# Adding the two halves of the attention's values by an accumulating transfer to DRAM

## The chip, the cores and the metric

The kernel runs on one core of a Trainium2 chip. The metric is the device time of one execution in microseconds (us), as the median of several runs. The engines are PE (TensorE, the matrix products), DVE (VectorE), ACT (ScalarE), POOL (GpSimd) and SP (SyncE, which here only issues transfers). Each engine works through its own queue in order and waits at semaphores for the others. Transfers are issued from SP's queue and, for some loads, from POOL's.

## The reference

Two layers (DEPTH = 2) run over 2048 latent tokens and 256 context tokens of width 1024. Each layer has multi-head latent attention with 8 heads (64 + 32 columns of query and key, 64 of value), a short convolution and a longer one; their outputs, each with a gate, go together through an output projection. Cut to the attention and what follows it:

```python
def one_block(qi):
    s = jnp.einsum('bqhd,bkhd->bhqk', qi, k).astype(jnp.float32) * sm_scale
    p = jax.nn.softmax(s, axis=-1).astype(v.dtype)
    return jnp.einsum('bhqk,bkhd->bqhd', p, v)
...
y_a = attn * jax.nn.silu(g_a)
...
return jnp.concatenate([y_a, y_b, y_c], axis=-1)
...
x <- x + gate * (y @ w_out[l])
```

In the last layer only the latent tokens are needed.

## The kernel before

Everything is in f32. To keep its precision, a product takes each operand as a rounded upper part and the remainder (names with h and l at the end: woh and wol, yh and yl, ph and pl), and the helper `mm3` makes three products of them (L194 to L196). The helper `split` makes the two parts: a cast on ACT (L190), then the subtraction of the remainder on POOL or DVE (L191).

Each layer has four stages: tokens, features, attention, project. The stages overlap at their ends: the project stage is written after the attention, but a raised priority lets its first part start 8 pairs (AE) before the attention ends.

**Attention.** Jobs run over 8 heads and, in each, over 4 blocks of 512 queries (layer 0 has a block of 256 context queries per head besides). A job walks through the 18 tiles of 128 keys in 9 pairs. For a pair PE makes the scores sc (L1080 to L1082), ACT takes two exponentials of them (p at L1083, the rounded ph at L1084), POOL subtracts the one from the other (pl, L1085), DVE adds p to the sums acc in PSUM (L1092), and, one pair later, PE multiplies ph and pl with the values (L1107, L1108) into po. The maxima of the next blocks are made ahead: PE makes a product pmax (L992), and DVE reduces it (mx, L993). The values stand in Vt with 128 columns: 64 of their upper part and 64 of the remainder. So po has 128 rows, and the attention's output is the sum of its rows 0 to 63 and 64 to 127.

The last pair of a job is followed by `close`: ACT copies the sums (accs, L1112) and po (o, L1114), SP stores o to DRAM (o_d, L1115), PE transposes the sums (L1120), and DVE makes their reciprocals (rinv, L1122 and L1123). What is to follow a pair is held in a list `late`, which `flush` empties after the next pair's subtraction.

**Project.** `prepare_w` loads a column of the output weights (wraw, L1150) and splits it into woh and wol. `prepare_y` loads, for one block of tokens, the gated outputs of the convolutions (L1170) and, per pair of heads k, both halves of o_d: the upper one into yr (L1175), the lower one into ylo (L1176), each in two transfers of 64 rows, and the gate yg (L1177). ACT and PE spread rinv over the rows (prr, L1181 and L1182). DVE then adds ylo to yr (L1183), multiplies by prr (L1184) and by the gate (L1185), and the result is split into yh and yl. The products pout (L194 to L196) follow; DVE adds them to the residual xo (L1213). In layer 0 the squares are summed for the next layer's norm, with the variance va at L1236 and its spreading on PE at L1243.

The order of each queue is not written out. A scheduler places all instructions by their priorities and its own estimate of times, and so a change in one place can move rows on any engine.

Of the kernel before, what the change touches and what calls it, by code (L numbers as in the profile page):

```python
# [9 lines left out]
F32 = mybir.dt.float32  # L10
# [3 lines left out]
ALU = mybir.AluOpType  # L14
# [4 lines left out]
P = 128  # L19
# [4 lines left out]
NT = SEQ + CTX  # L24
NTT = NT // P
DEPTH = 2
H = 8
NOPE, ROPE, DV, QK = 64, 32, 64, 96
# [56 lines left out]
def trunk(ctx: ExitStack, tc: tile.TileContext, ins, out):  # L85
    nc = tc.nc
    V, S, G, PE = nc.vector, nc.scalar, nc.gpsimd, nc.tensor

    def pool(stack, name, **kw):
        return stack.enter_context(tc.tile_pool(name=name, bufs=kw.pop("bufs", 1), **kw))  # L90
# [3 lines left out]
    dr = pool(ctx, "dr", space=DRAM)  # L94

    def psum(tag, name):
        return ps.tile([P, 512], F32, tag=tag, name=name, bufs={"a": 3, "b": 2}.get(tag, 1))
# [54 lines left out]
    v_d = [dr.tile([H, P, NTT, P], F32, name=f"v_d{l}") for l in range(DEPTH)]  # L152
    sga_d = [dr.tile([512, NT], F32, name=f"sga_d{l}") for l in range(DEPTH)]
    sgc_d = [dr.tile([256, NT], F32, name=f"sgc_d{l}") for l in range(DEPTH)]
    o_d = [dr.tile([H, P, NT], F32, name=f"o_d{l}") for l in range(DEPTH)]
    y_d = [dr.tile([512, NT], F32, name=f"y_d{l}") for l in range(DEPTH)]
    x1_d = dr.tile([D, NT], F32, name="x1_d")
    xs = [ins["xT"], x1_d]
# [780 lines left out]
    def attention(l, start):  # L939
# [3 lines left out]
        op = pool(es, f"Ao{l}", reuse_waits="tile", side="right")  # L943
# [29 lines left out]
        def bank(name):  # L973
            turns[0] += 1
            return psum("bbe"[turns[0] % 3], name)
# [71 lines left out]
        def use_mods():  # L1047
            while ready:
                i, j, parts = ready.pop(0)
                modulation(i, (j,), lambda _: parts, mp.tile([4, P], F32, tag="mrow", name="mrow", bufs=2))  # L1050


        late = []

        def flush():
            for st in late:
                st()
            late.clear()

        for idx, job in enumerate(jobs):  # L1060
            h = job[0][0]
            if job[0][1] == (1024 if h else 512) and h + 1 < H:
                load(h + 1)
            pairs = [(j, it) for j in job for it in range(j[3], NTT, 2)]
            for pi, ((h, s, n, k0), kt0) in enumerate(pairs):
                if idx == len(jobs) - 1 and pi == len(pairs) - AE:
                    mark = tc.cur_priority
                K, Vt, Q = kv[h]
                first, final = kt0 == k0, kt0 == NTT - 2
                if first:  # L1070
                    po = psum("c", "po")
                    acc = psum("d", "acc")
                p = tp.tile([P, 2, 512], F32, tag="p", name="p", bufs=4)
                ph = tp.tile([P, 2, 512], F32R, tag="ph", name="ph", bufs=3)
                pl = tp.tile([P, 2, 512], F32R, tag="pl", name="pl", bufs=3)
                scs = []
                for z in range(2):
                    kt, qt = kt0 + z, slice(s // P, (s + n) // P)
                    sc = psum("a", "sc")
                    PE.matmul(sc[:, :n], lhsT=K[0:97, kt, 0], rhs=Q[0:97, qt, 0], start=True, stop=False)  # L1080
                    PE.matmul(sc[:, :n], lhsT=K[0:QK, kt, 0], rhs=Q[0:QK, qt, 1], start=False, stop=False)  # L1081
                    PE.matmul(sc[:, :n], lhsT=K[0:QK, kt, 1], rhs=Q[0:QK, qt, 0], start=False, stop=True)  # L1082
                    S.activation(p[:, z, :n], sc[:, :n], AF.Exp, scale=scale)  # L1083
                    S.activation(ph[:, z, :n], sc[:, :n], AF.Exp, scale=scale)  # L1084
                G.tensor_tensor(pl[:, :, :n], p[:, :, :n], ph[:, :, :n].bitcast(F32), op=ALU.subtract)  # L1085
                flush()

                for z in range(2):
                    if first and z == 0:
                        V.tensor_copy(acc[:, :n], p[:, 0, :n])  # L1090
                    else:
                        V.tensor_tensor(acc[:, :n], acc[:, :n], p[:, z, :n], op=ALU.add)  # L1092
                for z in range(2):
                    at = pi + (z + 1) / 2 + LEAD
                    if at <= len(pairs):
                        ahead(idx + 1, at / len(pairs))
                    else:
                        ahead(idx + 1, 1)
                        ahead(idx + 2, (at - len(pairs)) / len(pairs))
                if pi == len(pairs) // 2:  # L1100
                    split_mods()
                if pi == len(pairs) - ME:
                    use_mods()

                def products(kt0=kt0, n=n, Vt=Vt, ph=ph, pl=pl, po=po, first=first, final=final):
                    for z in range(2):
                        PE.matmul(po[:, :n], lhsT=Vt[:, kt0 + z, :], rhs=ph[:, z, :n], start=first and z == 0, stop=False)  # L1107
                        PE.matmul(po[:, :n], lhsT=Vt[:, kt0 + z, :], rhs=pl[:, z, :n], start=False, stop=final and z == 1)  # L1108

                def close(h=h, s=s, n=n, po=po, acc=acc):  # L1110
                    accs = op.tile([P, 512], F32, tag="o", name="accs", bufs=3)
                    S.activation(accs[:, :n], acc[:, :n], AF.Copy, scale=2.0)  # L1112
                    o = op.tile([P, 512], F32, tag="o", name="o", bufs=3)
                    S.copy(o[:, :n], po[:, :n])  # L1114
                    nc.sync.dma_start(o_d[l][h, :, s : s + n], o[:, :n])  # L1115

                    nq = n // P
                    px = bank("psum_t")
                    for t in range(nq):
                        PE.transpose(out=px[:, t * P : (t + 1) * P], in_=accs[:, t * P : (t + 1) * P], identity=idn)  # L1120
                    sm = tp.tile([P, 4], F32, tag="sm", name="sm", bufs=2)
                    V.tensor_reduce(sm[:, :nq], px[:, :n].rearrange("p (t k) -> p t k", k=P), axis=AX.X, op=ALU.add)  # L1122
                    V.reciprocal(rinv[l][:, s // P : s // P + nq, h], sm[:, :nq])  # L1123

                late.append(products)
                if final:
                    late.append(close)
        if not AE:
            mark = tc.cur_priority
        flush()  # L1130
        if not last:
            assert not mods and not ready
            gains(l + 1)
# [4 lines left out]
    def project(l, start):  # L1138
# [3 lines left out]
        op = pool(es, f"Oo{l}", reuse_waits="tile", side="right")  # L1142
        rp = pool(es, f"Or{l}", reuse_waits="tile", side="right")
# [17 lines left out]
        def prepare_y(bi):  # L1161
            s, n = blocks[bi]
            where = (ap, bp)[bi % 2]
            yh = where.tile([P, KD, 512], F32R, tag="yh", name="yh")[:, :, :n]
            yl = where.tile([P, KD, 512], F32R, tag="yl", name="yl")[:, :, :n]
            ys[bi] = (yh, yl)
            for k in order:
                r = rp.tile([P, 512], F32, tag="yr", name="yr", bufs=4)
                if k >= 4:
                    nc.sync.dma_start(r[:, :n], y_d[l][(k - 4) * P : (k - 3) * P, s : s + n])  # L1170
                else:
                    lo = rp.tile([P, 512], F32, tag="ylo", name="ylo", bufs=2)
                    g = rp.tile([P, 512], F32, tag="yg", name="yg", bufs=2)
                    for z in range(2):
                        nc.sync.dma_start(r[64 * z : 64 * z + 64, :n], o_d[l][2 * k + z, 0:64, s : s + n])  # L1175
                        nc.sync.dma_start(lo[64 * z : 64 * z + 64, :n], o_d[l][2 * k + z, 64:128, s : s + n])  # L1176
                    nc.sync.dma_start(g[:, :n], sga_d[l][k * P : (k + 1) * P, s : s + n])  # L1177
                    px = psum("b" if bi == 0 else "cde"[k % 3], "prr")
                    for t in range(n // P):
                        rr = rp.tile([P, 2, 64], F32, tag="rr", name="rr", bufs=RR)  # L1180
                        S.copy(rr, rinv[l][:, s // P + t, 2 * k : 2 * k + 2].unsqueeze(2).to_broadcast([P, 2, 64]))  # L1181
                        PE.transpose(out=px[:, t * P : (t + 1) * P], in_=rr.rearrange("p a b -> p (a b)"), identity=idn)  # L1182
                    V.tensor_tensor(r[:, :n], r[:, :n], lo[:, :n], op=ALU.add)  # L1183
                    V.tensor_tensor(r[:, :n], px[:, :n], r[:, :n], op=ALU.mult)  # L1184
                    V.tensor_tensor(r[:, :n], r[:, :n], g[:, :n], op=ALU.mult)  # L1185
                split(yh[:, k, :n], yl[:, k, :n], r[:, :n], V if bi == 0 and (SPV & 4 and k < 4 or SPV & 8 and k >= 4) else None)
                yield
# [129 lines left out]
```

## Time and profile before

| | before |
|---|---|
| median of 3 runs | 3669.24 us (3668.04 to 3670.11) |
| the profiled execution | 3673.98 us |
| its span | 3672.2 us |
| mean granted clock of PE | 0.977 of 2.4 GHz |
| busy PE, DVE, POOL, ACT | 96%, 78%, 64%, 59% |
| moved by DMA, mean rate | 411.47 MB, 112 GB/s |

The profile is of one execution, by the hardware's own records. A row of the groups gives engine, operation and tiles (out<-in, buffer numbers left out), the count, then the busy time in us and the mean ns of one, then the time the engine stood idle just before such instructions and what ended it. A row of a timeline gives start and duration in us; several equal instructions in a row stand as xN, with their time together; square brackets give the idle time before it and its releaser. The span falls into these parts: layer 0's attention from 822 to about 1740 us, its projection up to about 1980, layer 1's tokens and features up to about 2620, its attention up to 3490 and its projection up to the end.

### The profile page before, as it was taken

Reading aid. Unit: us, or ns where it says so; the run is one execution under the profiler, and the core shown is the slowest. Engines: PE = TensorE matmul, PEld = TensorE weight load, DVE = VectorE, ACT = ScalarE, POOL = GpSimd, SP = SyncE. Lnnn points to the kernel's source line nnn. Section 1 sums busy time; section 2 is a strip of 40 time slices with the busy share of each in tenths; the row PEclk is TensorE's granted clock in tenths of the full one; section 3 lists DMA queues with packets and bytes.
Section 4 is the critical chain, followed back from the end, with each engine's and each line's share of the span. In section 5 each row is a group of like instructions: output and inputs, shape, how many; then the busy total and the mean of one; then the engine's idle time right before and its main releaser. Section 6 shows DMA issues by size and latency. Waiting matters only on the chain. (4 is left out here: it accounts for less than half of the span.)

```text
span 3672.2 us, 52697 instructions
## 1 busy us (share of the span) xinstructions
PE 3513.0 (96%) x17532; PEld 2913.7 (79%) x17532; DVE 2870.1 (78%) x5472; ACT 2167.6 (59%) x4328; POOL 2343.4 (64%) x1497
## 2 busy tenths in 40 slices
PE   7899999999999999999999989999999999999999
PEld 5787888887888888877788878887677888887777
DVE  6986977777888888887436879678988898888932
ACT  5665343337777877777445663433567777777720
POOL 4664344348888888887335664544678888887721
PEclk9899999999999999999999999999999999999999
DMA  7567333533333223311766773435241122222173
GB/s 220 172 186 208 82 108 103 119 105 88 80 80 80 50 65 80 87 55 46 239 216 208 219 225 91 132 91 134 66 97 29 43 62 59 62 59 72 40 207 115
DMA packets 394386, 411.47 MB, mean 112 GB/s; under 512 B 19168, under 2 KB 332128, under 8 KB 388960
## 3 DMA queue, kind: packets, MB, share of 16 engines
q1 hardware_dynamic: 387712, 333.87, 31.3%
q0 software_dynamic: 6400, 74.22, 8.9%
q8 instruction: 138, 2.26, 0.3%
q14 instruction: 136, 1.11, 0.1%
HBM read 266.72 MB, written 141.59 MB: 111 GB/s over the span
## 5 line engine op out<-in xcount | busy, mean ns | idle before, releaser
L1085 POOL TENSOR_TENSOR pl<-p,ph 128x1024 fp32r<-128x1024 f32 (+1 forms) x584 | 1389.4, 2391 | 262.4 <-ACT ph L1084 158.7
L1083 ACT ACTIVATE p<-sc 128x512 f32<-128x512 f32 x1168 | 704.7, 605 | 291.6 <-PE sc L1082 276.2
L993 DVE TENSOR_REDUCE mx<-pmax 128x1 fp32r<-128x512 f32 (+1 forms) x1296 | 787.0, 628 | 111.7 <-PE pmax L992 106.8
L1092 DVE TENSOR_TENSOR acc<-acc,p 128x512 f32<-128x512 f32 x1096 | 757.1, 691 | 66.8 <-ACT p L1083 44.8
L1084 ACT ACTIVATE ph<-sc 128x512 fp32r<-128x512 f32 x1168 | 698.3, 605 | 20.1 <-PE po L1107 16.4
L194 PE MATMUL pf<-hhf,wh 128*128 128x256 f32 (+1 forms) x1584 | 549.3, 348 | 16.8 <-ACT tg L867 8.3
L196 PE MATMUL pf<-hhf,wl 128*128 128x512 f32 (+1 forms) x1584 | 546.7, 347 | 3.9 <-POOL wl L191 2.9
L195 PE MATMUL pf<-hlf,wh 128*128 128x256 f32 (+1 forms) x1584 | 548.0, 346 | 0.2
L1080 PE MATMUL sc<-Q,K 97*128 97x512 f32 x1168 | 473.3, 405 | 8.6 <-ACT ph L1084 8.4
L992 PE MATMUL pmax<-K,Q 96*128 96x512 f32 (+1 forms) x1296 | 453.4, 384 | 26.4 <-DVE mx L993 19.6
L1108 PE MATMUL po<-pl,Vt 128*128 128x512 f32 x1168 | 466.3, 400 | 1.7 <-POOL pl L1085 1.0
L1081 PE MATMUL sc<-Q,K 96*128 96x512 f32 x1168 | 465.2, 398 | 0.0
L1107 PE MATMUL po<-ph,Vt 128*128 128x512 f32 x1168 | 461.1, 395 | 1.4 <-DMA Vt<-v_d 0.8
L1082 PE MATMUL sc<-Q,K 96*128 96x512 f32 x1168 | 462.0, 396 | 0.0
L191 POOL TENSOR_TENSOR wl<-wraw,wh 128x1024 fp32r<-128x1024 f32 x104 | 253.9, 2442 | 296.3 <-ACT wh L190 283.5
L747 DVE SCALAR_TENSOR_TENSOR cacc<-z,hv,cacc 128x384 f32<-128x384 f32 (+5 forms) x780 | 403.2, 563 | 14.3 <-ACT cacc L742 11.2
L194 PEld LDWEIGHTS pf<-hhf,wh 128*128 128x128 f32 x1584 | 303.9, 192 | 55.1 <-ACT tg L867 8.9
L196 PEld LDWEIGHTS pf<-hhf,wl 128*128 128x128 f32 x1584 | 303.4, 192 | 44.1 <-POOL wl L191 6.8
L195 PEld LDWEIGHTS pf<-hlf,wh 128*128 128x128 f32 x1584 | 304.2, 192 | 36.9 <-POOL hlf L191 0.6
L992 PEld LDWEIGHTS pmax<-K,Q 96*128 96x128 f32 x1296 | 244.7, 191 | 94.7 <-DVE mx L993 37.0
L1080 PEld LDWEIGHTS sc<-Q,K 97*128 97x128 f32 x1168 | 222.3, 190 | 61.6 <-ACT ph L1084 16.1
L1082 PEld LDWEIGHTS sc<-Q,K 96*128 96x128 f32 x1168 | 224.5, 192 | 51.4
(257 smaller groups left out, 6179.9 us busy)
## 6 DMA issues: line engine op xcount, KB each, us to landing
wraw<-in_w_in SPq DMA_DIRECT2D x108, 512.0 KB
q_d<-sg SPq DMA_DIRECT2D x68, 384.0 KB
wm<-in_w_mod SPq DMA_DIRECT2D x46, 512.0 KB
v_d<-vs SPq DMA_DIRECT2D x36, 512.0 KB
kn_d<-sg SPq DMA_DIRECT2D x72, 256.0 KB
K<-kn_d POOLq DMA_DIRECT2D x16, 1152.0 KB, 8.5
Vt<-v_d POOLq DMA_DIRECT2D x16, 1152.0 KB, 15.1
o_d<-o SPq DMA_DIRECT2D x64, 256.0 KB
```

The costliest lines, as they stand in the source:

```text
L194: PE.matmul(out_, lhsT=ahi, rhs=bhi, start=first, stop=False)
L195: PE.matmul(out_, lhsT=ahi, rhs=blo, start=False, stop=False)
L196: PE.matmul(out_, lhsT=alo, rhs=bhi, start=False, stop=last)
L992: PE.matmul(pm[:, :w], lhsT=Q[0:QK, s // P + t, 0], rhs=K[0:QK, a // P : (a + w) // P, 0], start=True, stop=True)
L993: V.tensor_reduce(part[:, t, c : c + 1], pm[:, :w], axis=AX.X, op=ALU.max)
L1080: PE.matmul(sc[:, :n], lhsT=K[0:97, kt, 0], rhs=Q[0:97, qt, 0], start=True, stop=False)
L1082: PE.matmul(sc[:, :n], lhsT=K[0:QK, kt, 1], rhs=Q[0:QK, qt, 0], start=False, stop=True)
L1083: S.activation(p[:, z, :n], sc[:, :n], AF.Exp, scale=scale)
L1084: S.activation(ph[:, z, :n], sc[:, :n], AF.Exp, scale=scale)
L1085: G.tensor_tensor(pl[:, :, :n], p[:, :, :n], ph[:, :, :n].bitcast(F32), op=ALU.subtract)
L1092: V.tensor_tensor(acc[:, :n], acc[:, :n], p[:, z, :n], op=ALU.add)
L1108: PE.matmul(po[:, :n], lhsT=Vt[:, kt0 + z, :], rhs=pl[:, z, :n], start=False, stop=final and z == 1)
```

## The change

The buffer o_d shrinks from 128 rows a head to 64. SP stores only the upper half of o. The lower half is added to it in DRAM by a transfer with `accum_op=ALU.add`, issued on POOL's queue. It can be issued only once the store has landed, so it is held in a list `adds` and issued by the third `flush` from the one that runs `close`, two pairs after it. In the project stage the loads of ylo, the tile and the addition L1183 are gone.

```diff
-    o_d = [dr.tile([H, P, NT], F32, name=f"o_d{l}") for l in range(DEPTH)]
+    o_d = [dr.tile([H, DV, NT], F32, name=f"o_d{l}") for l in range(DEPTH)]
...
+        adds = []
+
         def flush():
             for st in late:
                 st()
             late.clear()
+            for a in list(adds):
+                a[0] -= 1
+                if a[0] < 0:
+                    a[1]()
+                    adds.remove(a)
...
-                    nc.sync.dma_start(o_d[l][h, :, s : s + n], o[:, :n])
+                    nc.sync.dma_start(o_d[l][h, :, s : s + n], o[0:DV, :n])
+
+                    adds.append([2, lambda: G.dma_start(o_d[l][h, :, s : s + n], o[DV:P, :n], accum_op=ALU.add)])
...
-        flush()
+        while late or adds:
+            flush()
...
-                    lo = rp.tile([P, 512], F32, tag="ylo", name="ylo", bufs=2)
                     g = rp.tile([P, 512], F32, tag="yg", name="yg", bufs=2)
                     for z in range(2):
-                        nc.sync.dma_start(r[64 * z : 64 * z + 64, :n], o_d[l][2 * k + z, 0:64, s : s + n])
-                        nc.sync.dma_start(lo[64 * z : 64 * z + 64, :n], o_d[l][2 * k + z, 64:128, s : s + n])
+                        nc.sync.dma_start(r[64 * z : 64 * z + 64, :n], o_d[l][2 * k + z, :, s : s + n])
...
-                    V.tensor_tensor(r[:, :n], r[:, :n], lo[:, :n], op=ALU.add)
```

In counts: 72 accumulating transfers come onto POOL (40 in layer 0, 32 in layer 1; 64 of 512 columns and 8 of 256), 72 loads of 64 rows leave SP, 36 additions leave DVE. The new lines shift the numbers below them: in the changed kernel the subtraction pl is L1092, the sums acc L1099, the copies accs and o L1119 and L1121, the store L1122, the accumulation L1124, the loads of yr L1184, the multiplications L1191 and L1192, xo L1220.

Where instructions move: DVE at the end of layer 0's attention, before (yr and ylo belong to the project stage, mx and acc to the attention).

```order
L1123 RECIPROCAL rinv_63<-sm 128x2
L993 TENSOR_REDUCE mx_89<-pmax 128x1 x3
L1092 TENSOR_TENSOR acc<-acc,p 128x512
L993 TENSOR_REDUCE mx_89<-pmax 128x1
L1183 TENSOR_TENSOR yr<-yr,ylo 128x512
L993 TENSOR_REDUCE mx_89<-pmax 128x1
L1183 TENSOR_TENSOR yr<-yr,ylo 128x512
L1092 TENSOR_TENSOR acc<-acc,p 128x512
L993 TENSOR_REDUCE mx_89<-pmax 128x1 x3
```

The same place of the changed kernel:

```order
L1132 RECIPROCAL rinv_63<-sm 128x2
L993 TENSOR_REDUCE mx_89<-pmax 128x1 x2
L1099 TENSOR_TENSOR acc<-acc,p 128x512
L993 TENSOR_REDUCE mx_89<-pmax 128x1 x3
L1099 TENSOR_TENSOR acc<-acc,p 128x512
L993 TENSOR_REDUCE mx_89<-pmax 128x1 x3
L1099 TENSOR_TENSOR acc<-acc,p 128x512
```

The additions that stood between the maxima are gone, and maxima and sums close up.

ACT at the start of layer 1's projection, before (rr and woh and yh belong to the projection, the rest to the attention):

```order
L1181 COPY rr<-rinv_64 128x128 x3
L1112 ACTIVATE accs<-acc 128x512
L190 CAST woh<-wraw 128x1024
L1002 CAST Q<-pmt 1x4x128
L190 CAST yh<-yr 128x512 x2
L1114 COPY o<-po 128x512
L190 CAST yh<-yr 128x512 x2
```

And in the changed kernel:

```order
L1189 COPY rr<-rinv_64 128x128 x3
L1002 CAST Q<-pmt 1x4x128
L1119 ACTIVATE accs<-acc 128x512
L190 CAST woh<-wraw 128x1024
L190 CAST yh<-yr 128x512
L1090 ACTIVATE p<-sc 128x512
L1091 ACTIVATE ph<-sc 128x512
```

The cast of Q, which the next maxima need, has moved ahead of the copy of the sums and of the cast of woh, which waits for a load of weights.

POOL within layer 0's attention, in the changed kernel (wml is a split of modulation weights that runs beside the attention):

```order
L1092 TENSOR_TENSOR pl<-p,ph 128x1024 x5
L1124 DMA o_d_112<-o 64x512
L1092 TENSOR_TENSOR pl<-p,ph 128x1024 x5
L191 TENSOR_TENSOR wml<-wm,wmh 128x1024
L1092 TENSOR_TENSOR pl<-p,ph 128x1024 x4
L1124 DMA o_d_112<-o 64x512
```

Between two accumulations stand nine subtractions pl, one job; before, the same stretch held only the subtractions and the splits.

## Rows read from the trace of the kernel before

**Rows 1.** The page's part 1: busy us (share of the span), instructions.

```profile
PE 3513.0 (96%) x17532; PEld 2913.7 (79%) x17532; DVE 2870.1 (78%) x5472; ACT 2167.6 (59%) x4328; POOL 2343.4 (64%) x1497
```

**Rows 2.** Windows: length, busy us of PE, PEld, DVE, ACT, POOL, clock, DMA share, GB/s.

```profile
830.00:1600.00 770.00, 762.86 (x3783) 614.88 (x3782) 663.15 (x1244) 600.64 (x1129) 673.55 (x306) 1.00 0.30 72
1600.00:1760.00 160.00, 145.33 (x662) 113.00 (x661) 129.05 (x200) 111.37 (x230) 107.56 (x49) 0.94 0.26 80
```

**Rows 3.** Groups by line: count, then busy us, mean ns, then idle before and releasers.

```profile
L1183 DVE TENSOR_TENSOR yr<-yr,ylo 128x512 f32<-128x512 f32 (+1 forms) x36 | 38.3, 1063 | 65.6 <-DMA yr<-o_d 42.4 <-DMA ylo<-o_d 23.0
...
L1085 POOL TENSOR_TENSOR pl<-p,ph 128x1024 fp32r<-128x1024 f32 (+1 forms) x584 | 1389.4, 2391 | 262.4 <-ACT ph L1084 158.7 <-PE pmax L992 27.4 <-PE sc L1082 18.1
...
L1108 PE MATMUL po<-pl,Vt 128*128 128x512 f32 x1168 | 466.3, 400 | 1.7 <-POOL pl L1085 1.0
```

**Rows 4.** Timeline of DVE at the end of layer 0's attention: start, duration.

```profile
1622.63 6.68 DVE L1183 TENSOR_TENSOR yr<-yr,ylo 128x512 f32<-128x512 f32 x1 [0.90 <-DMA yr<-o_d]
1629.24 0.68 DVE L993 TENSOR_REDUCE mx<-pmax 128x1 fp32r<-128x512 f32 x1
1629.84 0.68 DVE L1183 TENSOR_TENSOR yr<-yr,ylo 128x512 f32<-128x512 f32 x1
```

**Rows 5.** Timeline of POOL at the same place.

```profile
1621.78 6.99 POOL L1085 TENSOR_TENSOR pl<-p,ph 128x1024 fp32r<-128x1024 f32 x3
```

**Rows 6.** Timeline of PE: five waits, and a reading of pl.

```profile
1629.97 0.58 PE L992 MATMUL pmax<-K,Q 96*128 96x256 f32 x1 [5.65 <-DVE mx L993]
...
1812.93 0.47 PE L1243 MATMUL prs<-idr,rep 128*128 128x128 f32 x2 [3.57 <-DVE rep L1242]
...
3367.58 0.80 PE L992 MATMUL pmax<-K,Q 96*128 96x512 f32 x1 [1.02 <-ACT Q L1002]
...
3385.95 1.10 PE L992 MATMUL pmax<-K,Q 96*128 96x512 f32 x2 [2.65 <-DVE mx L993]
...
3438.89 0.40 PE L1108 MATMUL po<-pl,Vt 128*128 128x512 f32 x1
...
3547.78 0.50 PE L194 MATMUL pout<-yh,woh 128*128 128x512 f32 x1 [1.24 <-DVE xo L1213]
```

**Rows 7.** Windows at three clock dips, and one after a store; columns as rows 2.

```profile
1626.70:1637.00 10.30, 7.03 (x17) 5.53 (x18) 9.46 (x13) 2.28 (x4) 2.93 (x2) 0.50 0.25 76
3367.50:3374.40 6.90, 6.82 (x18) 5.46 (x19) 4.20 (x8) 5.79 (x12) 6.16 (x5) 0.51 1.11 292
3388.00:3391.40 3.40, 3.40 (x10) 2.65 (x10) 3.39 (x6) 1.78 (x3) 0.00 (x0) 0.50 0.34 93
...
3236.60:3237.50 0.90, 0.90 (x5) 0.74 (x4) 0.64 (x2) 0.90 (x3) 0.00 (x0) 1.00 0.78 291
```

**Rows 8.** Timeline of DVE: layer 0's projection, and the start of layer 1's.

```profile
1807.75 0.69 DVE L1183 TENSOR_TENSOR yr<-yr,ylo 128x512 f32<-128x512 f32 x1 [5.10 <-DMA yr<-o_d]
...
3379.61 2.37 DVE L1183 TENSOR_TENSOR yr<-yr,ylo 128x512 f32<-128x512 f32 x1
3381.90 3.39 DVE L191 TENSOR_TENSOR wol<-wraw,woh 128x1024 fp32r<-128x1024 f32 x1
```

**Rows 9.** The chain that ended last, a piece in layer 1's projection: start, us, what.

```profile
3543.19 2.96 DMA ylo<-o_d
```

**Rows 10.** Groups by line: two of the four loads that POOL issues.

```profile
L967 POOL DMA_DIRECT2D Vt<-v_d x16 | 9.3, 584 | 3.0 <-PE pf L196 1.5 <-PE po L1108 0.9 <-PE pmax L992 0.6
...
L965 POOL DMA_DIRECT2D Q<-q_d x16 | 8.3, 522 | 0.0
```

**Rows 11.** Timeline of SP: three stores of o and a load of weights.

```profile
1655.47 0.33 SPq L1115 DMA_DIRECT2D o_d<-o  x1
...
1684.05 0.39 SPq L1150 DMA_DIRECT2D wraw<-in_w_out  x1
...
3235.81 0.32 SPq L1115 DMA_DIRECT2D o_d<-o  x1
...
3435.95 0.34 SPq L1115 DMA_DIRECT2D o_d<-o  x1
```

## The prediction

> **What bounds the kernel now.** I read the totals first: PE (TensorE) is busy 3513.0 of 3672.2 us, so the span is PE's work plus 159.2 us in which PE stands [rows 1]. Every other engine has room on the mean, so a microsecond taken from DVE or given to POOL counts only where PE waits for it. The windows then show where such places are. Inside the attention PE has no room left (762.86 of 770 us at clock 1.00) while POOL is at 673.55 of 770; at the change from the attention to the projection of layer 0 PE drops to 145.33 of 160 and the granted clock to 0.94 [rows 2]. The change takes work from DVE and SP, which act at those ends, and gives work to POOL inside the attention. So there are two sums: what PE's waits at the ends are worth, and what the new POOL work costs the full stretch.
>
> **What goes: 36 additions on DVE, 38.3 us** [rows 3]. A normal one takes 0.68 us (the last row of [rows 4]), but the mean is 1063 ns: some take much longer. All but a few lie beside PE's work, so I price only the five places where PE stood and an addition was in the way.
>
> Term 1, end of layer 0's attention. An addition takes 6.68 us, and the maximum (mx, L993) behind it starts at 1629.24 [rows 4]. On POOL three subtractions pl run without a gap over 1621.78 to 1628.77 [rows 5]; the addition ends 0.54 us after the last. So here a DVE instruction whose two inputs both come from SBUF stood until POOL let it in. The Trainium skill, "SBUF — State Buffer", section "Who interferes with whom", states such a rule: an operation of DVE with both inputs in SBUF contends with one of POOL that reads SBUF, and the second fully blocks; the trace agrees with 6.68 against 0.68 us. PE waits 5.65 us for that maximum [rows 6]. After it the granted clock is 0.50 over 1626.70 to 1637.00, the lower level of 1.2 GHz, and 7.03 us of PE work there would take 3.5 at the upper [rows 7]. Together 9.1 us. In the new order no addition is among these maxima; the sums acc between them read PSUM and one SBUF tile. What is late next is pl itself: POOL ends the subtractions of these pairs at 1628.77, and PE needs its products about then, so I take 9.1 and allow 4 as the low end.
>
> Term 2, projection of layer 0: an addition that waits for its load, at 1807.75, stands ahead of the last xo and of the variance va, and PE waits 3.57 us for what follows from va [rows 6, 8]. Without the 0.69 us addition and its load xo would start about 1 us earlier, as its matmuls are done. The multiplication L1191 still waits for a load there. I take 1.0, between 0 and 3.6.
>
> Term 3, start of the projection of layer 1: PE waits 1.02 us for Q of ACT [rows 6], then 6.82 us of work run at clock 0.51 [rows 7]: up to 1.02 + 3.4 = 4.4. In the new order of ACT the cast Q stands ahead of the cast of woh, which has to wait for a weight load. I take 3.0, between 0 and 4.4.
>
> Term 4, 18 us later: an addition of 2.37 us and the subtraction wol of 3.39 (both longer than the normal addition) hold the maxima back [rows 8]; PE waits 2.65 us [rows 6] and 3.40 us run at 0.50 [rows 7], up to 2.65 + 1.7 = 4.35. The addition goes and wol stays: 2.2, between 0 and 4.35.
>
> Term 5, projection of layer 1: the load of ylo takes 2.96 us, then come an addition and xo, and PE waits 1.24 us [rows 6, 9]. Load and addition go: 1.2.
>
> Sum 9.1 + 1.0 + 3.0 + 2.2 + 1.2 = 16.5 us; all five in full would be 22.7.
>
> With the additions go 72 loads (ylo) from SP, and the stores carry half the rows. SP isn't on PE's path except in terms 2 and 5, so I give nothing for it. Against that, the loads of yr now wait for an accumulation, and SP stands meanwhile, with all that is queued behind. The tightest is the last head's first block: in layer 0 its store goes at 1655.47, and the next transfer that somebody waits for, a weight load, at 1684.05 [rows 11]. The accumulation comes two pairs (about 5 us) and a landing later, so SP would stand some 8 us of these 28.6, and I price it at nothing; if the cover fails, it is the third rival.
>
> **What comes: 72 accumulating transfers on POOL.** None is in the trace. The nearest rows are POOL's own plain loads: 522 to 584 ns each, and the next POOL instruction starts behind them [rows 10]. At 0.55 us they hold POOL 40 us, at places where POOL mostly has spare time: 584 subtractions of 2391 ns leave it 262.4 us idle, and PE waited for pl just 1.0 us in all [rows 3]. Each accumulation also waits for its own store. The store of 3235.81 moves its data between 3236.60 and 3237.50 [rows 7, 11], 0.8 to 1.7 us after its issue, while the accumulation comes two pairs later. That covers the wait, except where SP issues the store late. One of the two tightest places is in layer 1: the store goes at 3435.95 and PE reads the next pl at 3438.89 [rows 6, 11], 2.9 us in which the landing, the accumulation and the pl no longer fit; my loss there is 1.7 us.
>
> I laid each of the 72 into POOL's rows at its new position, no earlier than 1.65 us after its store, and counted from the rows that rows 3 group what is left over once the gap ahead of the next pl, and the time from pl's end to PE's reading it, are used up (the median of the latter is 2.1 us). The last one or two of a layer I left out: behind them on POOL stand only the subtractions yl of the next block, hidden by the 192 products of the first; without that cover they would cost a landing each, 1.7 us. At 0.55 us each the loss is 4.2 us, at 1.0 it is 6.0, at 2.0 it is 11.5, at 2.5 it is 22.8, at 3.0 it is 45.2: flat as long as the cover holds, steep from there. The low end is zero (a gain has no ground: POOL only gets more). The high end is that POOL stands until the transfer has landed, 2.96 us by the load of the same shape [rows 9], so 45. I take 0.55 and 4.2, since rows 10 are the same instruction on the same engine. The Trainium skill, "DMA: Bandwidth & Descriptors", section "Anatomy of one DMA — SWDGE (gpsimd) path", gives a fixed 2.0 us for such a transfer and puts most of it into the landing; the 522 to 584 ns of rows 10 fit that reading. Were all 2.0 us POOL's, the estimate would be a loss of 11.5 in place of 4.2.
>
> **Sum.** The profiled execution took 3673.98 us, of which the span is 3672.2; it lies 4.7 above the median of the runs shown, 3669.24. 16.5 - 4.2 = 12.3 us less gives 3661.7 for the profiled execution and 3657 on the scale of the median.
>
> **Rivals.** *The accumulation holds POOL for long* (slower). If the issue costs 3 us, the loss of 45.2 against 16.5 makes 28.7 us more, 3698. It breaks even at about 2.2 us each and is slower by over 0.2% from about 2.5 us. For it: nothing shows what an accumulating transfer costs POOL, and POOL is at 87% in the attention [rows 2]. Against it: the two ends of rows 10 lie 62 ns apart, though one moves 96 rows and the other 128.
>
> *The stops only change their owner* (same). DVE's 38.3 us are off the path but for the ends. There, wol and the product with the gate (L1192) still have two SBUF inputs and still stand beside pl, and one late maximum is enough for a wait and a clock of 0.50. If terms 1, 3 and 4 give a third, 4.8 in place of 14.3, the sum is 4.8 + 2.2 - 4.2 = 2.8 us: 3666. For it: wol took 3.39 us without any addition's help [rows 8]. Against it: in term 1 no such operation stands near.
>
> *The new order makes stops of its own* (slower). Rows move on all engines from the first accumulation on. Two new stops of the size of term 1 (for instance SP standing at yr with the projection's weights behind it) and none of terms 1, 3, 4: 18.2 + 4.2 - 2.2 = 20.2 more, 3689.
>
> **How the numbers follow.** The forecast has a chance of 0.53, the change of owner 0.27, the dear accumulation 0.15, new stops 0.05. About 0.2% (7.3 us) is what a measurement of this kernel can tell from no change; 3657 lies beyond it, the second case within it, the others above it: faster 0.53, same 0.27, slower 0.20. The range reaches down to all five terms in full with a free accumulation (3669 - 22.7 = 3646.5) and 3 us more for an order that is luckier elsewhere, 3643. Upwards it takes in the second case and the cheaper half of the dear accumulation (2.5 to 2.8 us each), 3684.
>
> **What would show it.** Right: POOL rows of L1124 at about 0.55 us with pl directly behind; no addition on DVE; the wait of 5.65 us and the stretch at 0.50 after it gone; PE's wait for pl at L1108 grown by only a few microseconds, and PE's busy time down by some 7 us, as that is what the low clock added. Wrong: L1124 rows above 2 us, or a pl wait of tens of microseconds (first rival); the same idle sum on PE with wol, L1192 or SP's loads as releasers (second and third). The forecast falls if PE's idle time doesn't shrink at the two ends, whatever DVE saves.

## The result

The changed kernel takes 3786.8 us (median of 4 runs, 3775.61 to 3787.77) against 3669.68 us before: slower by 3.15%, ratio 1.0315 with a 95% interval of 1.0302 to 1.0328. I had forecast 3657 us, and the range ended at 3684.

The page's part 1 of the changed kernel, as [rows 1] of before:

```profile
PE 3536.7 (94%) x17532; PEld 2930.8 (78%) x17532; DVE 2833.0 (75%) x5436; ACT 2181.9 (58%) x4328; POOL 2398.0 (64%) x1569
```

Its span is 3773.6 us (the profiled execution, at 3775.61, is the fastest of the four). PE is idle for 236.9 us of it, 77.7 more than before, and busy for 23.7 more with the same 17532 products. DVE has lost 37 us of work and POOL has gained 55, and neither is near its limit. What PE waited for is in the view of its waits, the longest first (engine, line and tile; what released it; us in total, times, longest):

```profile
PE po L1115 <- POOL pl L1092: 84.6, 16, 7.6
PE px L403 <- DVE rawt L389: 14.6, 8, 2.8
```

This is the line that [rows 3] gave 1.0 us of waiting for pl. Its 83.6 us more are all of the added idle time; the other waits have together become some 6 us shorter. Why pl is late stands in POOL's waits:

```profile
POOL o_d L1124 <- DMA o_d<-o: 140.2, 15, 19.3
```

Fifteen of the 72 accumulations make POOL stand, 140.2 us in all, until the store of the upper half has landed, and every subtraction pl queued behind stands with it. Thirteen of the fifteen come right behind a round of POOL's loads for a coming head, one behind each of the thirteen rounds; the other two (10.45 and 1.71 us) are in the last blocks of the two layers, where no such loads run. One of the thirteen, in layer 1, on POOL's timeline:

```profile
2780.26 0.57 POOL L961 DMA_DIRECT2D K<-kn_d  x1
2780.83 0.55 POOL L962 DMA_DIRECT2D K<-kr_d  x1
2781.37 0.54 POOL L965 DMA_DIRECT2D Q<-q_d  x1
...
2790.12 0.60 POOL L967 DMA_DIRECT2D Vt<-v_d  x1
2790.74 4.76 POOL L1092 TENSOR_TENSOR pl<-p,ph 128x1024 fp32r<-128x1024 f32 x2
2803.74 0.89 POOL L1124 DMA_DIRECT2D o_d<-o  x1 [8.23 <-DMA o_d<-o]
2804.35 2.65 POOL L1092 TENSOR_TENSOR pl<-p,ph 128x1024 fp32r<-128x1024 f32 x1
```

SP and PE at the same place:

```profile
2788.77 0.45 SPq L1122 DMA_DIRECT2D o_d<-o  x1
```

```profile
2807.05 0.79 PE L1115 MATMUL po<-pl,Vt 128*128 128x512 f32 x1 [4.82 <-POOL pl L1092]
```

SP issued the store in time, at 2788.77. POOL got to the accumulation at 2795.5, and the store had not landed; it took until 2803.7, 15 us after its issue. Meanwhile the loads of keys, queries and values for a coming head, issued from 2780 on, were under way. The view of the DMA queues shows the two apart (q0 carries POOL's transfers, q1 SP's; packets, MB, share of the 16 engines). First from the store's issue to 2795.2, then from there to the accumulation:

```profile
q0 software_dynamic: 80, 1.16, 96.6%
```

```profile
q0 software_dynamic: 193, 1.72, 72.3%
q1 hardware_dynamic: 80, 0.13, 17.2%
```

For 6.4 us the loads hold the engines at 96.6% and not one packet of the store moves. Then its 0.13 MB go, between packets of the loads.

After such a wait PE's clock also falls. The window that begins just before the wait above ends (columns as in [rows 2]):

```profile
2806.20:2816.40 10.20, 9.35 (x34) 7.48 (x35) 4.89 (x9) 5.16 (x10) 10.19 (x5) 0.73 0.02 3
```

The mean granted clock is 0.73 there: the first part of the stretch is at the lower of its two levels (1.2 and 2.4 GHz), as the product above shows, which takes 0.79 us where 400 ns was the mean in [rows 3]. PE waits for pl sixteen times in all, and its busy time has grown by 23.7 us.

### The profile page after: what moved, and what is told of

It reads as the page before. It is cut to its first block, busy times and chain, and to the rows that moved or that the text cites. A ratio compares the mean times of both kernels' runs of the same rounds, so it can differ in the third digit from the quotient of the medians.

```text
span 3773.6 us, 52835 instructions
## 1 busy us (share of the span) xinstructions
PE 3536.7 (94%) x17532; PEld 2930.8 (78%) x17532; DVE 2833.0 (75%) x5436; ACT 2181.9 (58%) x4328; POOL 2398.0 (64%) x1569
## 5 line engine op out<-in xcount | busy, mean ns | idle before, releaser
L1092 POOL TENSOR_TENSOR pl<-p,ph 128x1024 fp32r<-128x1024 f32 (+1 forms) x584 | 1404.5, 2523 | 147.8 <-ACT ph L1091 85.7
L1099 DVE TENSOR_TENSOR acc<-acc,p 128x512 f32<-128x512 f32 x1096 | 757.7, 691 | 81.1 <-ACT p L1090 59.4
L1091 ACT ACTIVATE ph<-sc 128x512 fp32r<-128x512 f32 x1168 | 685.8, 603 | 66.3 <-PE po L1114 59.1
L1115 PE MATMUL po<-pl,Vt 128*128 128x512 f32 x1168 | 477.6, 409 | 85.3 <-POOL pl L1092 84.6
L1114 PE MATMUL po<-ph,Vt 128*128 128x512 f32 x1168 | 468.9, 401 | 0.8 <-DMA Vt<-v_d 0.8
L1115 PEld LDWEIGHTS po<-pl,Vt 128*128 128x128 f32 x1168 | 226.4, 194 | 145.9 <-POOL pl L1092 97.1
```

## The experiments

Two theories stood at the start. **A**: an accumulation makes POOL wait for its store, and stores that run beside the loads of a coming head land very late. **B**: the 72 transfers cost POOL too much, or the scheduler's new order makes stops of its own. Besides, the forecast gain of 16.5 us was to be measured alone.

**A longer hold in the list.**

```diff
-                    adds.append([2, lambda: G.dma_start(o_d[l][h, :, s : s + n], o[DV:P, :n], accum_op=ALU.add)])
+                    adds.append([6, lambda: G.dma_start(o_d[l][h, :, s : s + n], o[DV:P, :n], accum_op=ALU.add)])
```

> The changed kernel with one number altered: an accumulation is held back for six pairs after its store's block instead of two (about 16 us instead of 5). Theory A (the accumulation makes POOL wait for its own store, and that store lands 9 to 14 us late whenever the next head's loads fill the DMA engines): POOL's wait for the stores falls from 140 us to under 10, PE's wait for pl at L1115 from 84.6 us to under 8, and the time to 3655 to 3675. Theory B (72 more transfers cost POOL too much at 0.86 us each, or the new order makes its own stops): the waits stay, and the time stays above 3740.

Measured: 3785.08 us, ratio 1.0325 (1.0311 to 1.0339). That is no evidence for B: the rows of POOL, PE and DVE are in the same order as with 2. As I read this, the scheduler moves an instruction up to where it holds it ready, and by its estimate the store has landed soon, whatever the place in the program. So this was a second execution of the same order, and its waits are the same (POOL 152.1 us for the stores, PE 84.7 us for pl). The hold has to be a tie in POOL's own order; that is the fifth run.

**The same transfer without the adding.**

```diff
-                    adds.append([2, lambda: G.dma_start(o_d[l][h, :, s : s + n], o[DV:P, :n], accum_op=ALU.add)])
+                    adds.append([2, lambda: G.dma_start(o_d[l][h, :, s : s + n], o[DV:P, :n])])
```

> The changed kernel with the transfer of the lower half as a plain copy onto the same place in DRAM, so that it still has to wait for the store, but nothing is added; the upper half of the values is lost. Theory A (the wait for the store): 3770 to 3790 as with the accumulation, with POOL's wait for the stores at 130 to 150 us. Theory C (adding in DRAM is what costs time): below 3690, the accumulation's 0.86 us on POOL falling to the 0.55 us of a plain load.

Measured: 3776.8 us, ratio 1.03 (1.0283 to 1.0317). The wait is there without the adding:

```profile
POOL o_d L1124 <- DMA o_d<-o: 141.6, 16, 19.3
```

What the adding itself costs POOL is in the view of that line, of this kernel and then of the changed one (count, then minimum, median and maximum in ns):

```profile
L1124 POOL DMA_DIRECT2D o_d<-o x72: 542/557/563, 858.7 to 3593.9; - x72
```

```profile
L1124 POOL DMA_DIRECT2D o_d<-o x72: 806/855/1193, 855.9 to 3590.5; - x72
```

A plain store has the price that the loads of [rows 10] had, 0.56 us; an accumulation takes 0.3 us more. Theory C, that adding in DRAM is what costs, falls as the cause of the loss. The median is 10 us below the changed kernel's; whether these are the price of the adding is not shown.

**A store of POOL's own, without a wait.** The diff is against the kernel before; the smaller o_d and the list `adds`, as in the change, are cut from it.

```diff
...
+    o2_d = [dr.tile([H, DV, NT], F32, name=f"o2_d{l}") for l in range(DEPTH)]
...
-                    nc.sync.dma_start(o_d[l][h, :, s : s + n], o[:, :n])
+                    nc.sync.dma_start(o_d[l][h, :, s : s + n], o[0:DV, :n])
+                    adds.append([2, lambda: G.dma_start(o2_d[l][h, :, s : s + n], o[DV:P, :n])])
...
-                        nc.sync.dma_start(lo[64 * z : 64 * z + 64, :n], o_d[l][2 * k + z, 64:128, s : s + n])
+                        nc.sync.dma_start(lo[64 * z : 64 * z + 64, :n], o2_d[l][2 * k + z, :, s : s + n])
```

> The kernel before, but POOL stores the lower half to a buffer of its own, at the place and time where the change accumulates; DVE adds as before. So POOL has the 72 transfers, and none waits for SP's store. Theory A: 3669 to 3678, PE's wait for pl under 8 us. Theory B (POOL's time for 72 transfers, or the order): above 3700.

Measured: 3671.67 us against 3667.43, ratio 1.0009 (0.9999 to 1.0019). With 72 transfers on POOL that wait for no store of SP's, PE waits for pl 0.7 us in all:

```profile
PE po L1116 <- POOL pl L1093: 0.7, 1, 0.7
```

So the first half of B falls for transfers of 0.56 us, which are covered. That 0.86 us are covered too, and that the order isn't the cause, the fifth run shows.

**The removal alone.**

```diff
-                    lo = rp.tile([P, 512], F32, tag="ylo", name="ylo", bufs=2)
...
-                        nc.sync.dma_start(lo[64 * z : 64 * z + 64, :n], o_d[l][2 * k + z, 64:128, s : s + n])
...
-                    V.tensor_tensor(r[:, :n], r[:, :n], lo[:, :n], op=ALU.add)
```

> The kernel before without the loads of the lower half and the 36 additions, and without anything in their place (the lower half of the values is left out). It measures what the removal alone is worth. By the five terms of the prediction: 16.5 us less, about 3653. By the rival that the stops only change their owner: 3663 to 3670.

Measured: 3663.45 us against 3667.43, ratio 0.9993 (0.9985 to 1.0002): 4 us by the medians, of the 16.5, and the interval still includes no change at all. The wait of term 1 [rows 6] is gone, as I had it, and others have come. On DVE in layer 1, with POOL beside it and PE behind it:

```profile
3364.44 8.23 DVE L191 TENSOR_TENSOR wol<-wraw,woh 128x1024 fp32r<-128x1024 f32 x1
3372.60 1.87 DVE L993 TENSOR_REDUCE mx<-pmax 128x1 fp32r<-128x512 f32 x3
```

```profile
3362.23 9.36 POOL L1085 TENSOR_TENSOR pl<-p,ph 128x1024 fp32r<-128x1024 f32 x4
```

```profile
3373.33 0.79 PE L992 MATMUL pmax<-K,Q 96*128 96x512 f32 x1 [5.80 <-DVE mx L993]
```

The subtraction wol, also with two inputs from SBUF, now stands for 8.23 us until POOL's four pl are over; elsewhere in this kernel it takes 1.23. The same happens in layer 0 (6.53 us, PE waits 3.59). These are the stops with a new owner. The changed kernel itself has the one in layer 0, on DVE and PE:

```profile
1734.67 6.80 DVE L191 TENSOR_TENSOR wol<-wraw,woh 128x1024 fp32r<-128x1024 f32 x1
```

```profile
1741.60 0.58 PE L1001 MATMUL pmt<-idr,mx 128*97 128x128 f32 x2 [3.87 <-DVE mx L996]
```

Whether such a stop comes depends on the order: in layer 1 the changed kernel has none, with wol on DVE there too.

**The accumulation really held back.**

```diff
-                G.tensor_tensor(pl[:, :, :n], p[:, :, :n], ph[:, :, :n].bitcast(F32), op=ALU.subtract)
+                subs.append(G.tensor_tensor(pl[:, :, :n], p[:, :, :n], ph[:, :, :n].bitcast(F32), op=ALU.subtract))
...
-                    adds.append([2, lambda: G.dma_start(o_d[l][h, :, s : s + n], o[DV:P, :n], accum_op=ALU.add)])
+                    def add(h=h, s=s, n=n, o=o):
+                        with tc.issue_after(subs[-1].ins):
+                            G.dma_start(o_d[l][h, :, s : s + n], o[DV:P, :n], accum_op=ALU.add)
+                    adds.append([7, add])
```

> The changed kernel with each accumulation tied, in POOL's order, behind the subtraction pl of the pair that runs seven pairs after its block's end, so that it really comes some 20 us after its store (the count of two or six in the list moved nothing, since the scheduler places by readiness). Theory A (the wait for a store that lands 9 to 14 us late): POOL's wait for stores falls from 140 us to under 25, PE's wait for pl from 84.6 to under 8, the time to 3663 to 3675, since the removed additions alone were worth 4 us. Theory B (the dearer transfers or the scheduler's order): above 3720.

Measured: 3664.58 us against 3665.65, ratio 1.0001 (0.9990 to 1.0012). All of the 117 us are gone. POOL's wait and PE's:

```profile
POOL o_d L1126 <- DMA o_d<-o: 13.4, 2, 12.2
```

```profile
PE po L1115 <- POOL pl L1092: 0.9, 3, 0.4
```

Nearly all accumulations now come 15 to 23 us after their stores. The 12.2 us that remain are before the accumulation of the last latent block of layer 0, behind which no pl stands.

**The loads taken away, the accumulations left in place.**

```diff
         def load(h):
+            if h > 1:
+                kv[h] = kv[h - 2]
+                return
```

> The changed kernel as it is, accumulations where they were, but the keys, queries and values are loaded for the first two heads of a layer alone and used again for the others (14 of 16 loads of each kind left out, and the results of those heads with them). Nothing about the accumulations changes; only the traffic is gone that the late stores ran beside. Theory A: the stores land within 2 us everywhere, POOL's wait for them falls under 40 us (the first head's and the last blocks' remain), the time to 3655 to 3690. If the waits stay near 140 us and the time above 3760, the loads are not what makes the stores late.

Measured: 3670.22 us against 3665.65, ratio 1.0017 (1.0007 to 1.0027).

```profile
POOL o_d L1127 <- DMA o_d<-o: 32.0, 4, 19.2
```

The text says 14 of 16 loads; with eight heads in each of two layers it is 12 of 16 of each kind that are left out. The longest of the four waits that are left, 19.2 us, is in the first head of layer 1, while the second head's loads, which are still there, are under way. How soon the other stores landed is not measured by this, only that the accumulations no longer wait for them. The run also takes 48 issues off POOL, but 72 more cost next to nothing in the third run. With the fifth run this settles A from both sides: give the store time, or take the traffic away, and the loss goes.

**Two-input work off DVE at the ends.** With SPV = 0 the subtractions wol, and yl of the first block, run on POOL.

```diff
-SPV = 7
+SPV = 0
```

On the kernel of the fourth run:

> As the fourth run (no additions, no loads of the lower half, which is left out), and the subtractions that DVE makes for the output weights and the first block (wol, and yl of the first block) go to POOL too, so that no DVE instruction with two SBUF inputs stands among the maxima but the multiplication by the gate. If a DVE instruction blocked by POOL is what makes these stops, whichever it is, the stops of 5.8 and 3.6 us with a clock of 0.50 behind them vanish: 3650 to 3658. If POOL's extra work costs as much (it runs at 87% here): 3663 or more.

Measured: 3640.85 us against 3665.65 of the kernel before, ratio 0.9933 (0.9920 to 0.9946): 25 us, which is more than I expected. No stop of over 1.7 us is left at either end of the attention. One that went was no blocked maximum: at the start of layer 0's projection PE waited for ACT's copies rr, in the fourth run and, for comparison, in this one:

```profile
1739.29 3.06 PE L1180 MATMUL prr<-idr,rr 128*128 128x128 f32 x10 [5.84 <-ACT rr L1179]
```

```profile
1742.51 0.33 PE L1180 MATMUL prr<-idr,rr 128*128 128x128 f32 x1 [1.65 <-ACT rr L1179]
```

In the fourth run ACT stood at two casts of woh, 7.34 and 5.33 us, for loads of weights, ahead of these copies; here it doesn't. The longest wait of this kind is 5.8 us in the kernel before and 7.9 in the changed one. No term of the prediction priced it. Why the weights came late is not shown, nor how the 25 us divide among the stops. On the kernel of the fifth run:

> The held accumulation and the subtractions on POOL together, as a version that might beat both. If theory A holds and the seventh run gains: 3650 to 3665. If POOL is the limit with both: 3675 or more.

Measured: 3657.86 us, ratio 0.9980 (0.9971 to 0.9989). So once the stops at the ends are gone, the held accumulations cost 17 us beside a kernel that leaves the lower half out. PE waits for pl nowhere by more than a fraction of a microsecond in it. A part lies inside layer 0's attention, over 1200 to 1600 us, in the seventh run and then in this one:

```profile
1200.00:1600.00 400.00, 399.50 (x1980) 323.07 (x1979) 349.00 (x653) 315.21 (x595) 350.93 (x159) 1.00 0.26 64
```

```profile
1200.00:1600.00 400.00, 395.59 (x1952) 317.71 (x1951) 351.16 (x644) 312.10 (x587) 358.90 (x174) 1.00 0.30 65
```

PE gets through 28 products less, by my estimate some 6 us (28 at 0.2 us each); the rest is not taken apart. And on the kernel before:

> The kernel before, complete, with its DVE additions, and with the subtractions for the output weights and the first block on POOL instead of DVE; nothing of the change is in it. If wol on DVE is what held the maxima in the seventh run's comparison, most of that run's gain of 25 us is here too: 3640 to 3655. If the additions on DVE still get blocked beside pl and keep the stops: 3658 to 3668.

Measured: 3667.22 us against 3661.75, ratio 1.0010 (0.9998 to 1.0021). The addition now stands where wol stood. DVE, POOL and PE in layer 1:

```profile
3370.96 8.90 DVE L1183 TENSOR_TENSOR yr<-yr,ylo 128x512 f32<-128x512 f32 x1 [1.30 <-DMA yr<-o_d]
3379.78 1.27 DVE L993 TENSOR_REDUCE mx<-pmax 128x1 fp32r<-128x512 f32 x2
```

```profile
3367.68 7.03 POOL L1085 TENSOR_TENSOR pl<-p,ph 128x1024 fp32r<-128x1024 f32 x3
3374.68 2.33 POOL L191 TENSOR_TENSOR wol<-wraw,woh 128x1024 fp32r<-128x1024 f32 x1
3376.98 2.33 POOL L1085 TENSOR_TENSOR pl<-p,ph 128x1024 fp32r<-128x1024 f32 x1
```

```profile
3380.51 1.39 PE L992 MATMUL pmax<-K,Q 96*128 96x512 f32 x2 [8.59 <-DVE mx L993]
```

DVE stands for 8.90 us until POOL pauses at 3379.31, and PE waits 8.59 for the maximum behind. Neither half of the cure helps alone by more than the noise.

**Both on POOL, nothing in DRAM.** The ninth kernel with one more line changed; the whole computation is there.

```diff
-                    V.tensor_tensor(r[:, :n], r[:, :n], lo[:, :n], op=ALU.add)
+                    G.tensor_tensor(r[:, :n], r[:, :n], lo[:, :n], op=ALU.add)
```

> The ninth kernel with the 36 additions on POOL as well: the whole computation, nothing in DRAM, and neither the additions nor wol on DVE at the ends of the attention. If it takes both (no two-input work of DVE among the maxima) to be rid of the stops, as the fourth, seventh and ninth runs say together: 3640 to 3655, the stops of 5.6 and 8.6 us before pmax gone. If POOL's 45 us more at the ends delay pl or the first block's parts by as much: 3658 or more.

Measured: 3642.6 us against 3661.63, ratio 0.9948 (0.9933 to 0.9962). This version beats both kernels. The windows that [rows 2] showed at the end of layer 0's attention, and the one of layer 1, for it and then for the kernel before:

```profile
1600.00:1760.00 160.00, 155.60 (x725) 121.78 (x724) 106.84 (x187) 116.40 (x238) 145.09 (x73) 0.99 0.33 104
3350.00:3495.00 145.00, 141.70 (x630) 111.06 (x629) 98.82 (x158) 97.47 (x196) 127.71 (x63) 1.00 0.36 106
```

```profile
3350.00:3495.00 145.00, 137.79 (x583) 107.60 (x582) 124.64 (x188) 106.58 (x213) 110.04 (x48) 0.95 0.26 76
```

PE gets through 725 products in the first stretch where it was 662, and 630 in the second where it was 583, with the clock at 0.99 and 1.00 instead of 0.94 and 0.95. POOL is busier at both ends and doesn't hold PE up.

## Why the prediction was wrong

**The step that failed is the landing of the store.** I wrote that a store moves its data 0.8 to 1.7 us after its issue, read that from one store (3235.81, [rows 7, 11]), and replayed all 72 accumulations with 1.65 us. That store is the third block of a head, and no loads were under way. In the changed kernel it is about 14 to 19 us from the store's issue to the accumulation that waited for it wherever a round of loads was under way, and POOL's waits for stores sum to 140.2 us. The trace of before already held the others. The store of 2951.22, of the kernel before, with POOL's loads ahead of it:

```profile
2951.22 0.32 SPq L1115 DMA_DIRECT2D o_d<-o  x1
```

```profile
2942.90 0.54 POOL L961 DMA_DIRECT2D K<-kn_d  x1
...
2952.62 0.58 POOL L967 DMA_DIRECT2D Vt<-v_d  x1
```

The DMA queues from 2951.0 to 2957.5, then from 2957.5 to 2962.0:

```profile
q0 software_dynamic: 83, 1.21, 104.0%
```

```profile
q0 software_dynamic: 75, 0.83, 73.8%
q1 hardware_dynamic: 94, 0.18, 37.8%
```

Nothing of this store moves in the first 6.3 us, and its packets are still under way at 2962.0. Before the change nobody waited for it, and so no wait in the profile spoke of it. Scheduled transfers that nobody waits for have a cost that appears only with the first waiter. It recurs once a head, since the buffers for the loads come free at the end of a head, just when the last block's store goes out; the thirteen rounds of loads and their thirteen waits show it. For the accumulations that didn't stand for such a store, the replay's cover held. I haven't rerun it with the true landings; that it would have shown the loss is not shown.

**"Two pairs (about 5 us) later"** failed too. More than half of the accumulations start 2.8 to 3.7 us after their store's issue, so the list held them back by less than I had counted on, and no hold of 5 us covers a landing of 14 to 19. One of the early ones, on SP and POOL of the changed kernel:

```profile
1123.18 0.45 SPq L1122 DMA_DIRECT2D o_d<-o  x1
```

```profile
1125.95 0.85 POOL L1124 DMA_DIRECT2D o_d<-o  x1 [0.74 <-PE po L1115]
```

Some twenty start at this same distance of 2.8 us, POOL idle just before. That points to a quiet store counting as landed only then, and not at 1.65 us; the releaser named is another, so it is not shown.

**The price on POOL** was 0.55 us; it is 0.86. By the prediction's own sums 1.0 us each would have cost 6.0 us in place of 4.2. The rival of the dear accumulation named the right place (POOL's pl late, PE waiting at L1115) with the wrong cause: it set the breakeven at 2.2 us an issue, and the issue is far below. No rival had the wait for the store, though the change adds exactly that wait.

**The gain of 16.5 us** measured 4 by the medians, not clear of the noise (fourth run). Term 1's mechanism, a DVE instruction with two SBUF inputs that POOL keeps out, is right: it came again at 8.23 and 8.90 us. The Trainium skill's rule ("SBUF — State Buffer", "Who interferes with whom") agrees with both. The step that failed here is "what is late next": I named pl, where in the fourth run wol was next. The second rival had this: without the 4.2 us of accumulations its gain is 7.0 us, against 4 measured.

**What held**: the additions and their stops of term 1 are gone, POOL has room for the transfers, and the clock falls behind a long wait. The other Trainium skill rule that I set beside the rows ("DMA: Bandwidth & Descriptors", "Anatomy of one DMA — SWDGE (gpsimd) path") gives some 2 us for such a transfer, mostly its landing. An accumulation took 2.6 us from its issue to its landing at the least and 3.2 at the median, and held POOL for 0.86 of them, so the 2.0 us are not POOL's. One sum of the range doesn't come out: between 22.8 at 2.5 us and 45.2 at 3.0, a price of 2.8 us would end near 3689 and not at 3684. Nothing rests on it.

**The sum of the loss.** In the profiled executions, 101.4 us of span are 77.7 of PE's idle time (83.6 more for pl, the rest shorter by some 6) and 23.7 of busy time. The median is 11 us above the profiled execution of the changed kernel; the first run's profile, of the same order at 3786.7 us of span, has PE busy for 3546.5 us, 9.8 more, and idle for 240.2, so that difference is mostly PE's busy time. What makes it differ between executions is open. So is most of the 17 us between the seventh and eighth runs.

## What to carry to other kernels

A new wait for a transfer that nobody waited for before is priced by that transfer's worst landing in the trace, and that is read from the queue's packets at every recurrence, above all where large loads are under way. A row from a quiet stretch says nothing about the others. When work is taken off an engine where it blocks, look for the next instruction of the same kind on that engine: here the additions and the splits on DVE (wol, and yl of the first block) had to go together before anything clear of the noise was gained.

## What the runs showed of the hardware

- A store of 128 KB to DRAM, issued by SP, lay 6.4 us without a packet moving while loads of POOL's queue held the DMA engines at 96.6%, and took 15 us to land. With 12 of 16 of each kind of those loads left out, the accumulations waited 32.0 us in all for their stores instead of 140.2.
- An accumulating transfer held POOL 0.86 us at the median of 72 (64 of them of 64x512 f32), a plain one to the same place 0.56 us.
- A DVE subtraction of 1.23 us, with both inputs in SBUF, took 8.23 us beside four back-to-back instructions of POOL, and an addition of 0.68 us took 8.90.
